# A PEER gate build whose row products read one input from PSUM, with GpSimd making some of the weight splits beside them

## The chip, the cores and the metric

One Trainium2 chip, one of its cores. The metric is the device time of one execution in microseconds (us). The kernel before ran three times: 1541.89, 1541.98 and 1545.73 us, median 1541.98.

## What is computed

A decoder block for 512 tokens of width 1024 in fp32: LayerNorm, a hybrid mixer (Mamba-2 heads and latent attention), LayerNorm, and a PEER expert mixer, LayerNorm. The change lies in the PEER part:

```
q = (xb @ w_query).reshape(T, 8, 2, 128)
s = einsum('thkd,hknd->thkn', q, sub_keys)          # scores of 2 x 128 keys per head
sv, si = top_k(s, 16);  cand = sv[0] + sv[1]        # 256 candidates per head
top_s, pos = top_k(cand, 16);  gate = softmax(top_s)
expert e = 128 * i + j                              # 128 experts per token (8 heads x 16)
act  = gelu(x . u_table[e])
out += gate * act * v_table[e]                      # 16384 experts in the tables
```

## The kernel before

The tokens are four blocks of 128. For the first 384 tokens, less 64, the kernel doesn't gather experts: it multiplies by the whole tables. "U" is x times u_table, in 128 chunks of 128 experts for 320 tokens (`u_half`, L1395, two halves a chunk); "V" is the gated activations times v_table, in 128 chunks (`v_chunk`). A dense gate matrix is made for this from the selected experts in `build_g` (L1199). The last 64 tokens of block 2 get their activations from gathered rows: 64 gathers of 128 rows of 4 KB (`ug_fetch`, L1125, issued on GpSimd) and 64 products, a row tile times x, summed along the row on VectorE (`ug_dots`, L1131, the instruction is L1134). Block 3 is gathered in the same way later, in `gather` (L1518; products L1549 and L1555), beside the V chunks.

fp32 products are made of three fp32r matmuls (`mm3`, L84: high x high, high x low, low x high). The weights come through one `Stream` (L94): a DMA on the SP queue fetches a raw 128 x 1024 tile (three raw buffers), ScalarE copies it to fp32r (the high part `wih`, L122), and a subtraction raw minus high gives the low part `wil` (L132), on the engine that `lo_on` names: VectorE, or GpSimd in some earlier stages. The next raw tile's DMA is issued only when the subtraction has freed its buffer. A U chunk's low part is made when the chunk two before it starts.

`build_g` runs 48 iterations (n), each for 8 token columns of 384. An iteration has, on VectorE, the one-hot tile `oj` (L1222) and the gate tile `g` (L1228) for the next iteration, then two of the 64 gathered products (n < 32 only); on TensorE 16 small matmuls (L1264, L1265) into a ring of four PSUM tiles (`pw`), which ScalarE copies out (L1267). On GpSimd each product is followed by the gather of the row tile four ahead, as its buffer is then free (four row buffers, `UROWS`). At n = 9 and 25, `g_head` (L1166) transposes the next block's indices and gates into a PSUM tile (`px`, a second ring of two); `digits` (L1180) reads it at n = 11 and 27, `g_low` (L1189) at n = 12 and 28.

The order of the work is written out by a planner at build time, not chosen on the chip. `drive` (L1458) steps the generator `build_g`; it keeps two clocks, `tm[0]` for TensorE and `tm[1]` for VectorE, in us, and inserts U halves (1.8 us each on the first clock) while the first is not ahead of the second. A U chunk's low part adds 1.2 us to the second clock (L1453). An iteration with n < 32 yields twice: ahead of its two products, where halves come only if the clocks ask for them, and behind them, where at least one half is put. `drive` also stops inserting U at chunk 76 (`AHEAD`) or 85 (`PRE - RES`). Chunks up to 88 that are left when the build ends are run right behind it, ahead of the first V chunk, with block 3's gathered products pumped in between; the V loop starts with 88 chunks of U done in any case.

[...] The x of the 64 tokens lies in a strided part of an SBUF tile (`UR["x"]`, two DMAs at L1493, issued on GpSimd).

Of the kernel before, what the change touches and what calls it, by code (L numbers as in the profile page):

```python
# [11 lines left out]
F32 = mybir.dt.float32  # L12
# [5 lines left out]
AF = mybir.ActivationFunctionType  # L18
# [48 lines left out]
def tile_block(ctx: ExitStack, tc: tile.TileContext, I, out):  # L67
# [6 lines left out]
    def pool(name, bufs=1, **kw):  # L74
        p = tc.alloc_tile_pool(name=name, bufs=bufs, **kw)
        opened.append(p)
        return p
# [15 lines left out]
    class Stream:  # L93
# [32 lines left out]
        def splits(self, m):  # L126
            while self.ns < min(m, len(self.srcs)):
                n = self.ns
                self.his(n + 1 + self.ha)
                r, h = self.raw.pop(n), self.hi.pop(n)  # L130
                l = self.tiles(n, 1)[:, :r.shape[-1]]
                self.lo(n).tensor_tensor(l, r, h, op=OP.subtract)  # L132
                self.w[n] = (h, l)
                self.ns += 1
                self.loads(n + 1 + self.rawb)
# [119 lines left out]
    items = []  # L255
    plan = items.extend
    lo_on = [V]

    wo_ = [I["wo"][k] for k in range(16)]
    ut_ = [I["ut"][i] for i in range(128)]  # L260
# [666 lines left out]
    close(psT)  # L927
    close(cs2)

    psX = pool("psX", bufs=2, space=PSUM)  # L930
    psW = pool("psW", bufs=4, space=PSUM)
    px = lambda: psX.tile([128, 512], F32, name="px")
    pw = lambda: psW.tile([128, 512], F32, name="pw")

# [196 lines left out]
    def ug_dots():  # L1131
        for n in range(UG):
            r = UR.pop(n)
            V.scalar_tensor_tensor(wide(r), wide(r), 1.0, UR["x"], op0=OP.mult, op1=OP.mult, accum_out=UR["hd"][:, n:n + 1])  # L1134
            ug_fetch(n + UROWS)
            yield 1.2
        A.activation(UR["hd"][UG:], UR["hd"][UG:], AF.Gelu)
        nc.scalar.dma_start(UR["w"][:, UG:], UR["hd"][UG:])
        A.activation(UR["w"][:, :UG], UR["hd"][:UG], AF.Gelu)
        close(ug)  # L1140
        more_act(pool("act2"))
        yield 0.1

    def ug_head():
        w, g = UR["w"], UR["g"]
        mx, r = UR["m"][:, 0:1], UR["m"][:, 1:2]
        V.tensor_tensor(w, w, g, op=OP.mult)
        V.scalar_tensor_tensor(g, w, -1.0, w, op0=OP.mult, op1=OP.max)
        yield 0.6
        V.tensor_reduce(mx, g, axis=AX.X, op=OP.max)  # L1150
        V.tensor_scalar(mx, mx, 1.0e-30, None, op0=OP.max)
        V.reciprocal(r, mx)
        yield 0.7
        V.tensor_scalar(w, w, r, None, op0=OP.mult)
        G.dma_start(scl[128 - UG:], mx)
        yield 0.3
        ps = px()
        T.transpose(ps[:, :UG], w, ident[:UG, :UG])
        gT = GT[2][1][:, 64 - UG // 2:]
        gv = ps[:, :UG].rearrange("p (k c) -> p k c", c=2)  # L1160
        A.activation(gT[:, :, 0], gv, AF.Copy, scale=GSC)
        yield 0.1
        V.scalar_tensor_tensor(gT[:, :, 1], gv, GSC, gT[:, :, 0], op0=OP.mult, op1=OP.subtract)
        yield 0.2

    def g_head(b):  # L1166
        ijg = IJG.pop(b)
        ps = px()
        for x, e in enumerate((1, 2, 0)):
            T.transpose(ps[:, x * 128:(x + 1) * 128], ijg[:, e].rearrange("p h k -> p (h k)"), ident)  # L1170
        jT = ijp.tile([128, 64, 2], F16, name="jT", bufs=2)
        gT = ijp.tile([128, 64, 2, 2], F16, name="gT")
        rT = ijp.tile([128, 8, 4, 2], F32, name="rT", bufs=2)
        pr = ps[:, :384].rearrange("p (e k c) -> p e k c", e=3, c=2)
        A.activation(jT, pr[:, 0], AF.Copy)
        A.activation(gT[:, :, 0], pr[:, 1], AF.Copy, scale=GSC)
        GT["ps"] = pr, b
        GT[b] = jT, gT, rT
# [20 lines left out]
    def build_g():  # L1199
# [44 lines left out]
        for n in range(48):  # L1244
# [45 lines left out]
            if b < 2:  # L1290
                if g == 9:
                    g_head(b + 1)
                if g == 11:
                    digits()
                    lump += 0.9
                if g == 12:
                    g_low()
                    lump += 1.1
            lump += (1.45 if n + 1 in LOWA else 1.95) if n < 47 else 0.1
            if n < 32:  # L1300
                keep, least[0] = least[0], 0
                yield lump
                least[0], lump = keep, 0.0
            for _ in range(2):
                lump += next(dots, 0.0)
            for _ in range({35: 2, 36: 1, 37: 1, 38: 1}.get(n, 0)):
# [141 lines left out]
    def step_u():  # L1448
        e = len(UO)
        u_half(un[0], e)  # L1450
        un[0] += e
        tm[0] += T_U / 2
        if not e and lo_on[0] is V:  # L1453
            tm[1] += 1.2

    un = [uc]
# [1 line left out]
    def drive(fill):  # L1458
        n = 0
        while True:  # L1460
            if (tm[0] <= tm[1] and len(aps) == 1 or n < least[0]) and un[0] < (PRE - RES if len(aps) > 1 else AHEAD):
                step_u()
                n += 1
                continue
            c = next(fill, None)
            if c is None:
                return
            tm[1] += c
            n = 0
# [29 lines left out]
    iaE = rt2.tile([128, 16, 16], F16, name="iaE")  # L1499
    nc.sync.dma_start(iaE.rearrange("p a b -> p (a b)"), I["ch"][:, 256:512])  # L1500
    lo_on[0] = V
    drive(stage2())
    close(rt2)
    close(rt)
# [101 lines left out]
    refill()  # L1606
    if UO:
        step_u()
    close(psW)
    close(psX)  # L1610

    psV = pool("psV", space=PSUM)
    va = [[psV.tile([128, 512], F32, name=f"va{b}{e}") for e in range(2)] for b in range(3)]
# [262 lines left out]
```

## Time and profile before

| | us |
|---|---|
| median of 3 runs | 1541.98 |
| the profiled execution, whole | 1543.65 |
| its span in the trace | 1541.9 |
| TensorE matmul busy | 1520.9 (99%) |
| VectorE busy | 1354.3 (88%) |
| ScalarE busy | 761.0 (49%) |
| GpSimd busy | 644.3 (42%) |

All times below are us from the start of the span. The first small matmuls of the build's iteration 0 are at 599.05, those of iteration 32 at 806.49, and the build's last PSUM tile is copied out by 854. [...]

### The profile page before, as it was taken

To read this page: it belongs to the slowest core of one execution; us is meant where nothing else is said; L and a number is where in the kernel's file an instruction comes from. 1 tells how busy PE (TensorE), PEld (TensorE's weight loads), DVE (VectorE), ACT (ScalarE), POOL (GpSimd) and SP (SyncE) were. 2 spreads that over 40 slices of the span, in tenths; PEclk is the share of its full clock that TensorE was granted. 3 is DMA by queue.
4 is the path that set the end of the run, shared out by engine and by line. 5 is a ranking of instruction groups with operands and counts; after the bars stand their busy time and mean duration, and the time that the engine had idled before them with its cause. 6 is when DMAs were issued, how large, how long until landed. Compare 5 with 4: busy or idle time off the path is not lost.

```text
span 1541.9 us, 24586 instructions
## 1 busy us (share of the span) xinstructions
PE 1520.9 (99%) x8664; PEld 1339.1 (87%) x8664; DVE 1354.3 (88%) x2641; ACT 761.0 (49%) x1415; POOL 644.3 (42%) x469
## 2 busy tenths in 40 slices
PE   9999999999999999999999999999999999999997
PEld 7787888888888999999999889999999788888886
DVE  8989768746799999999998689999988999999997
ACT  5574477742433445667666544444443344444442
POOL 0000032520244422444430566666666677766610
PEclk9999999999999999999999999999999999999999
DMA  6242122474422566999998999999999999999983
GB/s 253 96 155 100 57 71 59 118 253 151 140 89 81 158 205 220 350 337 366 365 325 290 376 401 382 387 386 391 395 380 387 377 381 377 390 387 384 366 298 150
DMA packets 153452, 417.59 MB, mean 271 GB/s; under 512 B 15200, under 2 KB 56560, under 8 KB 153072
## 3 DMA queue, kind: packets, MB, share of 16 engines
q1 hardware_dynamic: 95568, 210.34, 39.3%
q0 software_dynamic: 52352, 187.25, 32.6%
q10 hardware_dynamic: 5408, 18.43, 3.0%
q8 instruction: 68, 1.11, 0.3%
q14 instruction: 56, 0.46, 0.1%
HBM read 383.59 MB, written 30.21 MB: 268 GB/s over the span
## 4 chain that ended last, share of the span: by engine, by line
PE 83%; DVE 6%; DMA 6%; issue 3%; ACT 2%; POOL 1%; DVEq 0%; ACTq 0%; POOLq 0%
PE va L1671 9%; PE va L1668 9%; PE va L1667 9%; PE pu L85 9%; PE pu L87 9%; PE pu L86 9%; PE pw L85 3%; PE pw L86 3%; PE pw L87 3%; PE pa L86 3%; PE pa L87 3%; PE pa L85 3%; DMA wir<-ut 2%; DMA row<-v,ix 2%; DMA row<-u,ix 2%
## 5 line engine op out<-in xcount | busy, mean ns | idle before, releaser
L122 ACT ACTIVATE wih<-wir 128x1024 fp32r<-128x1024 f32 (+2 forms) x269 | 277.7, 1033 | 191.9 <-DMA wir<-ut 87.9
L132 DVE TENSOR_TENSOR wil<-wir,wih 128x1024 fp32r<-128x1024 f32 (+1 forms) x232 | 280.7, 1211 | 76.4 <-ACT wih L122 50.1
L87 PE MATMUL pu<-XT,wil 128*128 128x320 f32 x1000 | 309.9, 310 | 0.2
L1668 PE MATMUL va<-wil,Ph 128*128 128x512 f32 x726 | 283.3, 390 | 1.4 <-DVE wil L132 1.4
L1534 POOL DMA_INDIRECT row<-v,ix x128 | 220.1, 1719 | 102.1 <-DVE ac L1555 81.1
L85 PE MATMUL pu<-XT,wih 128*128 128x320 f32 x824 | 257.6, 313 | 1.0 <-ACT aout L1409 1.0
L86 PE MATMUL pu<-XT,wih 128*128 128x320 f32 x824 | 254.5, 309 | 0.0
L1534 POOL DMA_INDIRECT row<-u,ix x128 | 181.3, 1416 | 133.7 <-DVE row L1549 72.9
L1667 PE MATMUL va<-wih,Ph 128*128 128x512 f32 x486 | 189.2, 389 | 0.0
L87 PEld LDWEIGHTS pu<-XT,wil 128*128 128x128 f32 x1000 | 188.3, 188 | 0.7 <-DVE wil L132 0.7
L1555 DVE SCALAR_TENSOR_TENSOR ac<-row,hd,ac 128x1024 f32<-128x1024 f32 x128 | 164.1, 1282 | 2.5 <-DMA row<-v,ix 0.9
L1668 PEld LDWEIGHTS va<-wil,Ph 128*128 128x128 f32 x726 | 136.3, 188 | 29.6 <-DVE wil L132 2.5
L85 PEld LDWEIGHTS pu<-XT,wih 128*128 128x128 f32 x824 | 154.7, 188 | 3.1 <-ACT aout L1409 1.3
L1549 DVE SCALAR_TENSOR_TENSOR row<-row,XT 128x1024 f32<-128x1024 f32 x128 | 153.3, 1224 | 3.2 <-DMA row<-u,ix 3.1
L86 PEld LDWEIGHTS pu<-XT,wih 128*128 128x128 f32 x824 | 154.8, 188 | 1.5
L1128 POOL DMA_INDIRECT urow<-u,uix x64 | 97.0, 1516 | 139.9 <-DVE urow L1134 120.5
L1671 PE MATMUL va<-wih,Pl 128*128 128x512 f32 x486 | 149.9, 389 | 1.9 <-DVE Pl L1658 1.9
L132 POOL TENSOR_TENSOR wil<-wir,wih 128x1024 fp32r<-128x1024 f32 (+3 forms) x37 | 77.8, 2110 | 144.8 <-ACT wih L122 125.4
L1650 ACT ACTIVATE Ph<-P 128x384 fp32r<-128x384 f32 x121 | 62.7, 518 | 125.8 <-DVE P L1627 110.1
L1671 PEld LDWEIGHTS va<-wih,Pl 128*128 128x128 f32 x486 | 91.2, 188 | 21.3 <-DVE Pl L1658 2.3
L1667 PEld LDWEIGHTS va<-wih,Ph 128*128 128x128 f32 x486 | 91.2, 188 | 18.1
L122 ACT ACTIVATE wihx<-wir 128x1024 fp32r<-128x1024 f32 x67 | 70.9, 1058 | 66.5 <-DMA wir<-v 38.3
(507 smaller groups left out, 3335.7 us busy)
## 6 DMA issues: line engine op xcount, KB each, us to landing
wir<-ut SPq DMA_DIRECT2D x128, 512.0 KB
wir<-v SPq DMA_DIRECT2D x128, 512.0 KB
gt<-gsp SPq DMA_DIRECT2D x63, 256.0 KB
wir<-wo SPq DMA_DIRECT2D x26, 512.0 KB
gsp<-stg ACTq DMA_DIRECT2D x21, 448.0 KB
wir<-wf SPq DMA_DIRECT2D x18, 512.0 KB
wir<-wqr SPq DMA_DIRECT2D x16, 512.0 KB
asp<-aout SPq DMA_DIRECT2D x35, 160.0 KB
```

What stands on the lines that cost most here:

```text
L85: T.matmul(ps, lh, rh, start=start, stop=False)
L86: T.matmul(ps, lh, rl, start=False, stop=False)
L87: T.matmul(ps, ll, rh, start=False, stop=stop)
L122: A.activation(h, r, AF.Copy)
L132: self.lo(n).tensor_tensor(l, r, h, op=OP.subtract)
L1128: G.indirect_dma_start(out=UR[n], out_offset=None, in_=I["u"], in_offset=bass.IndirectOffsetOnAxis(ap=UR["ix"][:, n:n + 1], axis=0))
L1534: G.indirect_dma_start(out=R[s], out_offset=None, in_=I["u"] if s < 128 else I["v"], in_offset=bass.IndirectOffsetOnAxis(ap=ix3[:, s % 128 ...
L1549: V.scalar_tensor_tensor(wide(r), wide(r), 1.0, x3, op0=OP.mult, op1=OP.mult, accum_out=hd[:, s:s + 1])
L1555: V.scalar_tensor_tensor(ac, r, hd[:, s - 128:s - 127], ac, op0=OP.mult, op1=OP.add)
L1667: T.matmul(va[b][e], Ph[b], h[:, cs], start=c == 0, stop=False)
L1668: T.matmul(va[b][e], Ph[b], l[:, cs], start=False, stop=False)
L1671: T.matmul(va[b][e], Pl[b], h[:, cs], start=False, stop=c == 127)
```

## The change

The input x of the 64 gathered products is copied once by ScalarE into two PSUM banks (the two of `px`, which is closed ahead of the build), and the products read it there. `g_head` and `ug_head` take a tile of the `pw` ring instead, and `digits` and `g_low` move to n = 10 and 26. Where a U chunk starts at the first yield of an iteration with n < 32, its low part is made by GpSimd: VectorE first writes one column of the low tile (a memset of 128 x 1), so that GpSimd's subtraction starts where VectorE has come to that place in its order, just ahead of the two products; the planner's VectorE clock is not charged for it.

```diff
--- before.py
+++ after.py
@@ -129,7 +129,11 @@
                 self.his(n + 1 + self.ha)
                 r, h = self.raw.pop(n), self.hi.pop(n)
                 l = self.tiles(n, 1)[:, :r.shape[-1]]
-                self.lo(n).tensor_tensor(l, r, h, op=OP.subtract)
+                if beside[0]:
+                    V.memset(l[:, 0:1].bitcast(F32), 0.0)
+                    G.tensor_tensor(l, r, h, op=OP.subtract)
+                else:
+                    self.lo(n).tensor_tensor(l, r, h, op=OP.subtract)
                 self.w[n] = (h, l)
                 self.ns += 1
                 self.loads(n + 1 + self.rawb)
@@ -255,6 +259,7 @@
     items = []
     plan = items.extend
     lo_on = [V]
+    beside = [False]
 
     wo_ = [I["wo"][k] for k in range(16)]
     ut_ = [I["ut"][i] for i in range(128)]
@@ -927,8 +932,8 @@
     close(psT)
     close(cs2)
 
+    psW = pool("psW", bufs=4, space=PSUM)
     psX = pool("psX", bufs=2, space=PSUM)
-    psW = pool("psW", bufs=4, space=PSUM)
     px = lambda: psX.tile([128, 512], F32, name="px")
     pw = lambda: psW.tile([128, 512], F32, name="pw")
 
@@ -1131,7 +1136,7 @@
     def ug_dots():
         for n in range(UG):
             r = UR.pop(n)
-            V.scalar_tensor_tensor(wide(r), wide(r), 1.0, UR["x"], op0=OP.mult, op1=OP.mult, accum_out=UR["hd"][:, n:n + 1])
+            V.scalar_tensor_tensor(r, r, 1.0, UR["xp"], op0=OP.mult, op1=OP.mult, accum_out=UR["hd"][:, n:n + 1])
             ug_fetch(n + UROWS)
             yield 1.2
         A.activation(UR["hd"][UG:], UR["hd"][UG:], AF.Gelu)
@@ -1154,7 +1159,7 @@
         V.tensor_scalar(w, w, r, None, op0=OP.mult)
         G.dma_start(scl[128 - UG:], mx)
         yield 0.3
-        ps = px()
+        ps = pw()
         T.transpose(ps[:, :UG], w, ident[:UG, :UG])
         gT = GT[2][1][:, 64 - UG // 2:]
         gv = ps[:, :UG].rearrange("p (k c) -> p k c", c=2)
@@ -1165,7 +1170,7 @@
 
     def g_head(b):
         ijg = IJG.pop(b)
-        ps = px()
+        ps = pw()
         for x, e in enumerate((1, 2, 0)):
             T.transpose(ps[:, x * 128:(x + 1) * 128], ijg[:, e].rearrange("p h k -> p (h k)"), ident)
         jT = ijp.tile([128, 64, 2], F16, name="jT", bufs=2)
@@ -1290,17 +1295,16 @@
             if b < 2:
                 if g == 9:
                     g_head(b + 1)
-                if g == 11:
+                if g == 10:
                     digits()
                     lump += 0.9
-                if g == 12:
                     g_low()
                     lump += 1.1
             lump += (1.45 if n + 1 in LOWA else 1.95) if n < 47 else 0.1
             if n < 32:
-                keep, least[0] = least[0], 0
+                keep, least[0], beside[0] = least[0], 0, True
                 yield lump
-                least[0], lump = keep, 0.0
+                least[0], lump, beside[0] = keep, 0.0, False
             for _ in range(2):
                 lump += next(dots, 0.0)
             for _ in range({35: 2, 36: 1, 37: 1, 38: 1}.get(n, 0)):
@@ -1450,7 +1454,7 @@
         u_half(un[0], e)
         un[0] += e
         tm[0] += T_U / 2
-        if not e and lo_on[0] is V:
+        if not e and lo_on[0] is V and not beside[0]:
             tm[1] += 1.2
 
     un = [uc]
@@ -1499,6 +1503,11 @@
     iaE = rt2.tile([128, 16, 16], F16, name="iaE")
     nc.sync.dma_start(iaE.rearrange("p a b -> p (a b)"), I["ch"][:, 256:512])
     lo_on[0] = V
+    close(psX)
+    psG = pool("psG", space=PSUM)
+    UR["xp"] = psG.tile([128, D], F32, name="xp")
+    for e in range(2):
+        A.activation(UR["xp"][:, e * 512:(e + 1) * 512].rearrange("p (a b) -> p a b", b=64), UR["x"][:, e * 8:(e + 1) * 8], AF.Copy)
     drive(stage2())
     close(rt2)
     close(rt)
@@ -1606,8 +1615,8 @@
     refill()
     if UO:
         step_u()
+    close(psG)
     close(psW)
-    close(psX)
 
     psV = pool("psV", space=PSUM)
     va = [[psV.tile([128, 512], F32, name=f"va{b}{e}") for e in range(2)] for b in range(3)]
```

## Rows read from the trace of the kernel before

**Rows 1.** Busy time by stretch of us, the granted clock, the DMA share.

```profile
core 0: us, PE busy (x) PEld busy (x) DVE busy (x) ACT busy (x) POOL busy (x), PEclk, DMA share, GB/s
599.00:806.50 207.50, 204.88 (x1689) 200.64 (x1687) 199.45 (x275) 136.09 (x288) 92.92 (x68) 0.99 0.95 342
806.50:853.60 47.10, 47.10 (x461) 45.60 (x460) 40.66 (x49) 33.15 (x67) 2.46 (x5) 1.00 0.84 296
866.00:1186.00 320.00, 320.00 (x1707) 285.45 (x1706) 287.77 (x422) 140.80 (x255) 211.81 (x163) 1.00 1.02 389
1186.00:1240.00 54.00, 50.47 (x259) 43.07 (x258) 49.17 (x52) 19.86 (x35) 36.79 (x24) 1.00 1.01 376
```

**Rows 2.** TensorE's busy time and granted clock in two stretches of 2 us.

```profile
752.00:754.00 2.00, 2.00 (x10) 0.50 1.01 404
754.00:756.00 2.00, 2.00 (x11) 0.68 1.03 340
```

**Rows 3.** Waits in 599 to 806.5: who waited for whom, total, times, longest.

```profile
ACT wih L122 <- DMA wir<-ut: 22.2, 12, 4.6
DVE wil L132 <- ACT wih L122: 4.6, 4, 1.6
PE pu L85 <- ACT aout L1409: 2.6, 2, 1.6
DVE urow L1134 <- DMA urow<-u,uix: 1.0, 3, 0.5
```

**Rows 4.** Line L1288, all its instructions: columns of U already done, times 32.

```profile
L1288 DVE TENSOR_TENSOR acts<-acts,stg x10: 1086/1616/1628, 625.7 to 832.7; 128x1408 f32<-128x1408 f32 x7, 128x896 f32<-128x896 f32 x1, 128x1152 f32<-128x1152 f32 x1, 128x1280 f32<-128x1280 f32 x1
```

**Rows 5.** Timelines of GpSimd and ScalarE where x is fetched; a small DMA's wait.

```profile
527.16 1.70 POOL L1493 DMA_DIRECT2D XT<-xsp  x2
...
528.13 0.44 ACT L1406 ACTIVATE acts<-pu 128x320 f32<-128x320 f32 x1 [2.13 <-PE pu L87]
...
531.65 0.44 ACT L1406 ACTIVATE acts<-pu 128x320 f32<-128x320 f32 x1 [2.13 <-PE pu L87]
...
555.41 1.87 POOL L1128 DMA_INDIRECT urow<-u,uix  x1 [3.52 <-DMA uix<-p]
```

**Rows 6.** Timeline of VectorE around the first pair of products.

```profile
599.79 1.22 DVE L1134 SCALAR_TENSOR_TENSOR urow<-urow,XT 128x1024 f32<-128x1024 f32 x1
600.93 1.22 DVE L1134 SCALAR_TENSOR_TENSOR urow<-urow,XT 128x1024 f32<-128x1024 f32 x1
602.08 1.22 DVE L132 TENSOR_TENSOR wil<-wir,wih 128x1024 fp32r<-128x1024 f32 x1
603.22 0.69 DVE L1222 TENSOR_TENSOR oj<-iotaE,jT 128x1024 f16<-128x1024 f16 x1
```

**Rows 7.** Whole span, by group: a memset, inputs in PSUM, in SBUF.

```profile
L383 DVE MEMSET cu<- 128x3 f32 x12 | 0.7, 61 | 0.0
L976 DVE TENSOR_TENSOR XT<-px,XT 128x512 fp32r<-128x512 f32 x8 | 5.2, 687 | 1.3 <-ACT XT L975 1.3
L504 DVE TENSOR_TENSOR xdt<-xs,dtt 128x512 f32<-128x512 f32 x8 | 5.1, 685 | 0.0
```

**Rows 8.** Timeline of GpSimd and of VectorE beside two low parts.

```profile
397.57 4.78 POOL L132 TENSOR_TENSOR wil<-wir,wih 128x1024 fp32r<-128x1024 f32 x2 [81.16 <-ACT wih L122]
...
397.24 1.28 DVE L960 SCALAR_TENSOR_TENSOR xm<-hres,pu 128x512 f32<-128x512 f32 x2
...
400.56 1.81 DVE L188 SCALAR_TENSOR_TENSOR lma<-lmy,lmh 128x1 f32<-128x1 f32 x1
...
402.60 0.22 DVE L188 SCALAR_TENSOR_TENSOR lma<-lmy,lmh 128x1 f32<-128x1 f32 x1
```

**Rows 9.** A gather on GpSimd, and the product that waited for its row.

```profile
607.90 1.44 POOL L1128 DMA_INDIRECT urow<-u,uix  x1 [0.30 <-issue]
...
617.09 1.23 DVE L1134 SCALAR_TENSOR_TENSOR urow<-urow,XT 128x1024 f32<-128x1024 f32 x1 [0.51 <-DMA urow<-u,uix]
```

**Rows 10.** GpSimd's instructions by group, whole span: gathers of the build.

```profile
L1128 POOL DMA_INDIRECT urow<-u,uix x64 | 97.0, 1516 | 139.9 <-DVE urow L1134 120.5 <-issue 8.8 <-DMA urow<-u,uix 7.1
```

## The prediction

> **What bounds the kernel now.** I read the busy time by stretch first, then the waits of the build, then the timelines of VectorE and GpSimd inside it. The stretches show that TensorE is the clock of the whole kernel: 320.00 of 320 us busy from 866 to 1186, 47.10 of 47.1 in the build's last third, 204.88 of 207.5 in its first 32 iterations (n < 32), which the change rewrites [rows 1]. [...] The other hole is at 1186 to 1240, 54.00 - 50.47 = 3.5 us [rows 1].
>
> So shorter work on VectorE is worth nothing by itself. The most that can be had is the idle time that the change can reach, 2.6 + 1.7 + 3.5 = 7.8 us; the only way to lose is new idle time on TensorE. The question is therefore whether the other engines still keep up when the planner gives TensorE less to do in the build.
>
> In n < 32 all are close together: VectorE is busy 199.45 of 207.5 us and the DMA engines at a share of 0.95 [rows 1].
>
> **What the planner does with it.** I worked its two clocks through with the costs in the code. For the kernel before this gives 28, 36, 40 and then 44 chunks of U done at the gate multiplications; the rows have 896, 1152, 1280 and 1408 columns, 32 times these, so the working holds [rows 4]. For the change it gives: 38 U chunks in n < 32 in place of 48, of which 19 get their low part on GpSimd (the title counts 16), and 77 chunks at the end of the build in place of 85. The 19 stand in n = 2, 4 to 10, 13, 14, 17, 20 to 22, 25, 26 and 28 to 30. The U work that leaves the build is not saved: it runs behind it at the same price.
>
> **TensorE's floor.** A chunk takes 531.65 - 528.13 = 3.52 us [rows 5]. Iterations 0 to 31 take 806.49 - 599.05 = 207.4 us, without holes and slow clock 207.4 - 2.6 - 1.7 = 203.1. Ten chunks fewer: 203.1 - 35.2 = 167.9 us.
>
> **VectorE.** 48 subtractions become 19: 29 fewer at 602.08 - 600.93 = 1.15 us from start to start (a duration of 1.22 overlaps its neighbour) [rows 6], 33.3 us. Added: 19 memsets at 0.06 [rows 7], 1.1 us. The trace has no product of 1024 columns with an input in PSUM. With 512 columns such an instruction takes 687 ns, one with both inputs in SBUF 685 [rows 7], so the lower end is nothing; the pair of products with a PSUM input beside GpSimd came at 0.64 us each [rows 8], against half of 1.15, which bounds the extra at 0.07 per 512 columns, 0.14 x 63 = 9 us. A fixed extra per instruction wouldn't double with the columns, so I take 0.05 x 63 = 3 us. VectorE then needs 199.5 - 33.3 + 1.1 + 3 = 170.3 us (167 to 176), a little over TensorE's floor, with no wait in it. Before, it had about 6 us of waits [rows 3].
>
> [...]
>
> **DMA.** 0.95 x 207.5 = 197 us of the engines' time. Ten chunks fewer are 5.2 MB of weights and 1.6 MB of stored activations, at 342 / 0.95 = 360 GB/s 19 us: 178 us are left. At the later rate, 389 / 1.02 = 381 GB/s, what moved here, 71 MB less 6.8, takes 168 us [rows 1]. So DMA is level with TensorE or 10 us beyond it; I don't expect the waits for weights (22.2 us on ScalarE, 12 times [rows 3]) to go.
>
> **GpSimd, the step that decides.** A low part takes 4.78 / 2 = 2.39 us there [rows 8]; the two gathers of an iteration take 1.52 us each [rows 10] and about 0.30 of issue in front [rows 9]: 2.39 + 2 x 1.82 = 6.0 us an iteration where GpSimd has all three. On average it fits (19 x 2.39 + 64 x 1.82 = 162 us), in runs it doesn't. In n = 4 to 10 the planner gives TensorE 37.2 us by its clock, x 203.1 / 209.4 (real to planned in the kernel before) = 36.1 us, and GpSimd needs 7 x 6.0 = 42.0: 5.9 late. In n = 20 to 22 and 28 to 30 it is 18.0 against 15.7 each time, 2.3 late. Together 10.5 us. Queued behind a late low part are the two gathers, and for their rows wait the products two iterations on, with all of VectorE behind them. That cover is thin: one row was used 617.09 - 607.90 = 9.2 us after its gather was issued and VectorE still waited 0.5 us [rows 9], while the iterations shrink from 6.5 to 5.2 us, so two of them leave 10.5 less the pair itself.
>
> A low part that starts late also overhangs the products. What that does is in the trace: beside two low parts the instruction with one PSUM input ran unhindered, while one of a single column with two SBUF inputs took 1.81 us, to the end of the low part, in place of 0.22 [rows 8]. In the build that is `oj`, `g` or the next subtraction. [...]
>
> TensorE has up to two iterations of `oj` and `g` ahead of it, so the first microsecond or so of each run is absorbed: I take 8 of the 10.5 (3 to 16, the upper end with 19 x 6.0 + 13 x 5.2 = 182 against 168, and 2 more of waiting).
>
> **The rest.** *x into PSUM:* ScalarE's two copies wait for two DMAs that GpSimd issues at 527.2 to 528.9; a small one took 3.5 us to land, a gather 9.2 [rows 5, 9], so ScalarE goes on at 533 to 539, two copies of some 0.6 us included. TensorE has a second U tile and waits only when the evacuation of 531.65 is 3.5 us late, past 535.2: 0 to 4 us, taken as 1. *Transposes in `pw`:* the fifth tile after them waits until VectorE has read the transposes, two digits calls at up to 2 us; `digits` stands right behind the one-hot tile that TensorE needs anyway: 0 to 4, taken as 0.5. *After the build:* 11 chunks stand ahead of V in place of 3, 9 of them with products of block 3 pumped beside them in place of 1, some 15 of 256 done earlier. That thins the load at 1186 to 1240 by 6%; of the 3.5 us there I take 1.5 back (0 to 3.5).
>
> **Sum.** n < 32: 167.9 + 8 (GpSimd's runs; VectorE's excess of 2.4 lies inside them) + 2.6 + 1.7 (waits for weights and slow clock as before) = 180.2. With the moved chunks 180.2 + 35.2 - 207.4 = +8.0; + 1 + 0.5 - 1.5: +8.0 us on the span of 1541.9. The profiled execution took 1543.65, 1.7 above the median; on the median of 1541.98 it makes 1550.
>
> **Rivals.**
> 1. *The cover holds, and TensorE never waits* (faster, 0.23). Place: the second gather of an iteration with a GpSimd low part. If it is issued in time for its row to be there two iterations on, VectorE at its lower end (167) keeps pace, the 2.6 + 1.7 us go, and up to 3.5 later: 1534 to 1538. For it: VectorE waited only 1.0 us for rows, in 3 products [rows 3]. Against: 6.0 us of GpSimd in iterations of some 5. It decides at a row latency of about 8 us.
> 2. *Nothing but a shift* (0.17). The new idle time equals what the old stalls give back: 1540 to 1545.
> 3. *The raw tiles come late* (0.15). The next weight DMA goes out only when the subtraction has freed its raw buffer; on GpSimd that is 2.39 - 1.15 = 1.2 us later at best, 3 to 4 behind two gathers. Where ScalarE already waited up to 4.6 us for a tile [rows 3], 19 x 1.2 to 19 x 1.9 us (with the upper end of VectorE included) fall on TensorE: +16 to +32, 1558 to 1574. Products that hold GpSimd's reading after all would end here too.
> 4. *The change doesn't do what it says:* the planner's choice is fixed in the code, so only the title's 16 or my 19 can be off; 16 would take 1.5 us from the sum.
>
> **Chances.** The forecast (GpSimd late in its runs) 0.45, with its own range 1544 to 1557; the rivals 0.23, 0.17 and 0.15. 0.3% is 4.6 us, about what a measurement tells from no change: below 1537.4 faster, above 1546.6 slower. Faster: rival 1, 0.23, and a little of rival 2, 0.25. Same: most of rival 2 and the lower end of the forecast, 0.25. Slower 0.50. The range reaches from the middle of rival 1 to the lower part of rival 3: 1536 to 1565.
>
> **What would show it.** Right: gathers in n = 4 to 10 issued one after the other with no wait for a product; waits of products for rows well over 1.0 us; TensorE idle by some 10 us in the build; stretches of granted clock under 1. The product's start-to-start time tells the PSUM term (1.15 to 1.3). Wrong: TensorE busy throughout n < 32 and that stretch at 168 to 170 us (rival 1), or ScalarE's wait for weights far over 22 us with TensorE behind it (rival 3). [...]

## The result, and the profile after

The change is slower: median 1563.61 us of 4 runs (1561.61 to 1565.36) against 1543.86 for the kernel before (4 runs), ratio 1.0114 (95% interval 1.0076 to 1.0151). The profiled execution took 1561.61 us, its span is 1559.6: 17.7 us longer than before, where 8.0 was forecast. On the medians it is 19.8 us longer. The median lies at the upper end of the range, 1536 to 1565, and 6.6 us above the forecast's own range, 1544 to 1557.

First the stretches of the changed kernel (columns as in [rows 1]). Its iterations n < 32 are the first row; the others are the build's next part, the first part of the V stage, its start alone, a later part of it, and the place where x is fetched.

```profile
606.20:783.90 177.70, 172.58 (x1420) 164.04 (x1418) 163.09 (x257) 118.30 (x262) 115.98 (x78) 0.99 0.95 351
783.90:830.00 46.10, 44.16 (x416) 42.28 (x417) 41.28 (x51) 31.85 (x65) 7.04 (x13) 1.00 0.82 285
860.00:1180.00 320.00, 317.49 (x1711) 283.69 (x1710) 280.30 (x411) 145.32 (x263) 193.62 (x151) 1.00 1.00 380
860.00:890.00 30.00, 27.49 (x170) 25.34 (x169) 25.71 (x37) 13.33 (x24) 17.99 (x15) 1.00 1.03 412
1180.00:1240.00 60.00, 60.00 (x332) 54.23 (x331) 56.94 (x59) 23.14 (x38) 43.91 (x27) 1.00 1.02 387
520.00:560.00 40.00, 35.53 (x226) 35.26 (x225) 35.84 (x98) 18.12 (x27) 9.64 (x9) 0.91 0.55 149
```

By the busy times, TensorE idled 2.6 us before in n < 32 and, in the other stretches of [rows 1], only at 1186 to 1240. Now it idles 5.1 us in n < 32, 4.5 ahead of it, 1.9 behind it and 2.5 between 860 and 890. The hole at 1186 to 1240 is gone.

A correction to a mark of the prediction belongs here. Counting the gate matmuls, 16 to an iteration, the kernel before starts n = 32 at 803.74; 806.49 is n = 33. Its n < 32 therefore took 204.7 us, not 207.4, and the forecast for it, by the same steps, 204.7 - 2.6 - 1.7 - 35.2 = 165.2 and 8 + 2.6 + 1.7 = 12.3 on it, becomes 177.5 in place of 180.2. Expectations below that name such lengths were written with the old marks, up to an iteration off; the tables here use the counted ones.

With it the span splits at three starts: the first gate matmul, that of n = 32, the first V matmul.

| part of the span, us | before | after | difference | forecast |
|---|---|---|---|---|
| to n = 0 | 599.1 | 606.2 | +7.2 | +1 |
| n < 32 | 204.7 | 177.7 | -27.0 | -27.2 |
| n = 32 to the first V matmul | 60.2 | 101.6 | +41.4 | +35.2 + 0.5 |
| V to the end | 678.0 | 674.1 | -3.9 | -1.5 |

The parts of one kernel differ from run to run: two more profiles of the change (e5 and e12 below) have 176.8 and 179.0 in n < 32, and 676.7 and 674.8 from V to the end.

**Ahead of the build.** The timelines of ScalarE and GpSimd, after:

```profile
534.95 1.23 ACT L1510 ACTIVATE xp<-XT 128x512 f32<-128x512 f32 x2 [8.45 <-DMA XT<-xsp]
536.12 0.42 ACT L1410 ACTIVATE acts<-pu 128x320 f32<-128x320 f32 x1
...
527.67 1.71 POOL L1497 DMA_DIRECT2D XT<-xsp  x2
```

(`xp<-XT` are the two copies of x into PSUM, `XT<-xsp` the two DMAs that fetch x.) ScalarE stands in front of its copies for 8.45 us; x lands 7.3 us after GpSimd began to issue the two DMAs. No U tile (`pu`) is evacuated from then to 536.12. What that does to TensorE is in stretches of 2 us (after; the first busy time is TensorE's, the third number from the end its granted clock as a share of full speed):

```profile
532.00:534.00 2.00, 0.12 (x1) 0.00 (x0) 2.00 (x4) 0.00 (x0) 0.00 (x0) 1.00 0.88 173
534.00:536.00 2.00, 0.00 (x0) 0.00 (x0) 1.93 (x4) 1.02 (x2) 1.33 (x1) 0.75 0.81 229
536.00:538.00 2.00, 1.41 (x5) 1.41 (x6) 0.44 (x2) 2.00 (x5) 0.00 (x0) 0.50 0.80 184
538.00:540.00 2.00, 2.00 (x10) 2.00 (x9) 0.80 (x1) 1.98 (x2) 0.00 (x0) 0.50 0.67 141
540.00:542.00 2.00, 2.00 (x10) 2.00 (x10) 1.20 (x3) 1.97 (x3) 0.00 (x0) 0.55 0.66 238
```

It is idle from 532.12 to 536.59, 4.5 us, and comes back at a granted clock of 0.50, a U matmul every 0.267 us in place of 0.147, until shortly before 542: (1.41 + 2.00) x 0.50 + 2.00 x 0.45 = 2.6 us of full speed more. Together 7.1, the table's first line.

**In n < 32.** The waits after, 606 to 784 (columns as in [rows 3]):

```profile
ACT wih L122 <- DMA wir<-ut: 13.7, 8, 3.2
DVE urow L1139 <- DMA urow<-u,uix: 13.1, 15, 2.1
DVE wil L136 <- ACT wih L122: 1.1, 1, 1.1
ACT g L1237 <- DVE g L1233: 16.0, 11, 3.0
PE pu L85 <- ACT aout L1413: 1.6, 1, 1.6
PE pw L1269 <- DVE g L1233: 1.4, 1, 1.4
PE pw L1269 <- DVE wil L133: 1.0, 1, 1.0
```

Products wait for their rows 13.1 us in 15 places, against 1.0 in 3 [rows 3]. VectorE's 163.1 us of work, these 13.1 and 1.1 of waiting for a high part make 177.3 of the 177.7: VectorE is the bound here, and TensorE waits for its `g` and for what stands behind the late rows. (In the two other profiles of the change the rows wait 7.8 and 9.4 us.) GpSimd's timeline shows why rows are late, from 638 on:

```profile
638.53 2.41 POOL L134 TENSOR_TENSOR wil<-wir,wih 128x1024 fp32r<-128x1024 f32 x1 [2.02 <-ACT acts L1410]
641.09 0.94 POOL L1133 DMA_INDIRECT urow<-u,uix  x1 [0.15 <-issue]
642.34 1.35 POOL L1133 DMA_INDIRECT urow<-u,uix  x1 [0.30 <-DVE units L1219]
643.71 2.38 POOL L134 TENSOR_TENSOR wil<-wir,wih 128x1024 fp32r<-128x1024 f32 x1
646.26 1.22 POOL L1133 DMA_INDIRECT urow<-u,uix  x1 [0.16 <-issue]
647.78 0.95 POOL L1133 DMA_INDIRECT urow<-u,uix  x1 [0.30 <-issue]
648.75 2.40 POOL L134 TENSOR_TENSOR wil<-wir,wih 128x1024 fp32r<-128x1024 f32 x1
```

Low part, gather, gather, low part, with hardly anything between but issue, until 659.8: some 5.3 us an iteration (6.0 forecast), and none of these gathers waits for a product. VectorE beside it:

```profile
644.54 1.22 DVE L1139 SCALAR_TENSOR_TENSOR urow<-urow,xp 128x1024 f32<-128x1024 f32 x1
...
645.69 0.97 DVE L1227 TENSOR_TENSOR oj<-iotaE,jT 128x1024 f16<-128x1024 f16 x1
...
650.01 1.70 DVE L1227 TENSOR_TENSOR oj<-iotaE,jT 128x1024 f16<-128x1024 f16 x1
...
654.13 1.22 DVE L1139 SCALAR_TENSOR_TENSOR urow<-urow,xp 128x1024 f32<-128x1024 f32 x1 [0.68 <-DMA urow<-u,uix]
656.03 1.22 DVE L1139 SCALAR_TENSOR_TENSOR urow<-urow,xp 128x1024 f32<-128x1024 f32 x1 [0.67 <-DMA urow<-u,uix]
```

The products with x in PSUM run at 1.22 us through a low part. `oj`, two inputs in SBUF, takes 0.97 and 1.70 in place of 0.69 [rows 6] where the low part is still under way (643.71 + 2.38 = 646.09; 648.75 + 2.40 = 651.15). Soon after, two rows in turn are late.

How a late row reaches TensorE stands in the timelines of VectorE, ScalarE and TensorE around 643:

```profile
640.44 1.22 DVE L1139 SCALAR_TENSOR_TENSOR urow<-urow,xp 128x1024 f32<-128x1024 f32 x1 [0.92 <-DMA urow<-u,uix]
...
642.79 0.68 DVE L1233 TENSOR_TENSOR g<-tens,units 128x1024 f16<-128x1024 f16 x1
...
643.51 2.48 ACT L1237 ACTIVATE g<-g,rT 128x128 f16<-128x128 f16 x8 [5.04 <-DVE wil L133]
...
643.53 0.23 PE L1269 MATMUL pw<-g,oj 128*128 128x128 f16 x1 [1.02 <-DVE wil L133]
...
644.29 0.22 PE L1270 MATMUL pw<-g,oj 128*128 128x128 f16 x1
...
644.58 0.22 PE L1270 MATMUL pw<-g,oj 128*128 128x128 f16 x1
```

The product waits for its row, `g` behind it ends at 643.47, and TensorE stands until then. (The wait is put down to `wil`, a memset beside it; it is `g` that the matmul reads.) Where `g` has 1024 columns, ScalarE makes its other half in eight small copies (L1237), and TensorE now runs at their pace: one pair of gate matmuls in 0.29 us (644.29 to 644.58) in place of 2 x 0.0585. The waits don't list these steps, as each is short.

**Ahead of V.** Eleven U chunks now stand between the build and V. ScalarE's timeline there, after:

```profile
874.70 1.06 ACT L122 ACTIVATE wihx<-wir 128x1024 fp32r<-128x1024 f32 x1 [2.64 <-DMA wir<-ut]
878.88 1.06 ACT L122 ACTIVATE wih<-wir 128x1024 fp32r<-128x1024 f32 x1 [2.80 <-DMA wir<-v]
883.05 1.06 ACT L122 ACTIVATE wih<-wir 128x1024 fp32r<-128x1024 f32 x1 [2.78 <-DMA wir<-v]
```

These high parts come every 4.18 us (4.0 on average from 862.93 on), each after waiting for its raw tile, where a chunk takes TensorE 3.52. Block 3's rows are fetched beside them, and the DMA share of 860 to 890 is 1.03. TensorE loses 3.1 us between 860 and 886, counted as below. The SP queue and TensorE there:

```profile
873.71 0.33 SPq L104 DMA_DIRECT2D wir<-v  x1
...
882.47 0.33 SPq L104 DMA_DIRECT2D wir<-v  x1
...
880.32 0.41 PE L85 MATMUL pu<-XT,wihx 128*128 128x320 f32 x1 [0.40 <-ACT aout L1413]
...
885.54 0.50 PE L1676 MATMUL va<-wih,Ph 128*128 128x512 f32 x1 [1.44 <-ACT Ph L1659]
```

The raw tile whose DMA is issued at 873.71 is taken at 883.05, 9.3 us later. The DMA of 882.47 goes out when the subtraction of 881.22 has freed its buffer, 3.6 us after that buffer's tile was taken at 878.88. With three buffers that makes (9.3 + 3.6) / 3 = 4.3 us a tile, an estimate near the 4.18. TensorE's waits are named after ScalarE's evacuation and its `Ph`, which stand behind the waiting high parts in ScalarE's order.

### The profile page after: what moved, and what is told of

It reads as the page before. It is cut to its first block, busy times and chain, and to the rows that moved or that the text cites. A ratio compares the mean times of both kernels' runs of the same rounds, so it can differ in the third digit from the quotient of the medians.

```text
span 1559.6 us, 24660 instructions
## 1 busy us (share of the span) xinstructions
PE 1530.6 (98%) x8664; PEld 1343.6 (86%) x8664; DVE 1337.6 (86%) x2641; ACT 759.8 (49%) x1417; POOL 655.0 (42%) x488
## 4 chain that ended last, share of the span: by engine, by line
PE 79%; DMA 8%; DVE 7%; issue 3%; ACT 2%; POOL 1%; ACTq 0%; DVEq 0%; POOLq 0%
PE va L1677 10%; PE va L1676 10%; PE va L1680 10%; PE pu L85 7%; PE pu L87 7%; PE pu L86 7%; DMA urow<-u,uix 4%; PE pw L85 3%; PE pw L86 3%; PE pw L87 3%; PE pa L86 3%; PE pa L87 3%; PE pa L85 3%; DMA wir<-v 1%; PE pb L533 1%
## 5 line engine op out<-in xcount | busy, mean ns | idle before, releaser
L136 DVE TENSOR_TENSOR wil<-wir,wih 128x1024 fp32r<-128x1024 f32 (+1 forms) x218 | 263.6, 1210 | 91.4 <-ACT wih L122 45.9
L1543 POOL DMA_INDIRECT row<-v,ix x128 | 210.7, 1646 | 124.8 <-DVE ac L1564 100.8
L1543 POOL DMA_INDIRECT row<-u,ix x128 | 173.4, 1354 | 156.1 <-DVE row L1558 92.1
L1133 POOL DMA_INDIRECT urow<-u,uix x64 | 79.1, 1236 | 73.9 <-DVE urow L1139 60.8
```

The source lines that it names most:

```text
L1133: G.indirect_dma_start(out=UR[n], out_offset=None, in_=I["u"], in_offset=bass.IndirectOffsetOnAxis(ap=UR["ix"][:, n:n + 1], axis=0))
L1543: G.indirect_dma_start(out=R[s], out_offset=None, in_=I["u"] if s < 128 else I["v"], in_offset=bass.IndirectOffsetOnAxis(ap=ix3[:, s % 128 ...
```

## The experiments

Holes are counted alike in all kernels: over TensorE's matmul starts, the distance to the next start less the ordinary distance (0.147 us for a U matmul, 0.0585 for a gate matmul). Slow clock is in them. Without its holes n < 32 is 197.6 us in kernels with 72.5 U chunks done at n = 32, and 162.4 with 62.5: ten chunks less, 35.2 us. Of the change's 15.3 us in n < 32, some 6 are the steps at ScalarE's pace described above, 5.9 single waits over 0.25 us; before, there are none of the first and 2.9 of the second.

| | U chunks at n = 32 | holes to n = 0 | in n < 32 | n = 32 to V | V to end, us | span |
|---|---|---|---|---|---|---|
| before | 72.5 | 0.5 | 7.1 | 1.0 | 678.0 | 1541.9 |
| the change | 62.5 | 7.2 | 15.3 | 7.2 | 674.1 | 1559.6 |
| e1 late copy | 62.5 | 1.4 | 19.1 | 6.5 | 674.1 | 1557.6 |
| e2 no GpSimd low part | 72.5 | 0.6 | 4.1 | 2.1 | 676.7 | 1539.7 |
| e3 planner charged | 72.5 | 0.5 | 6.3 | 4.1 | 675.3 | 1542.1 |
| e4 products from SBUF | 62.5 | 0.5 | 42.4 | 6.6 | 675.1 | 1580.8 |
| e5 the change again | 62.5 | 7.1 | 14.5 | 7.6 | 676.7 | 1562.6 |
| e6 credit alone | 62.5 | 0.6 | 22.4 | 6.6 | 674.1 | 1560.4 |
| e7 low part behind the gathers | 62.5 | 0.9 | 39.1 | 6.7 | 675.1 | 1578.0 |
| e8 six rows | 62.5 | 1.0 | 9.6 | 10.6 | 675.3 | 1552.8 |
| e9 charged, six rows | 72.5 | 0.6 | 2.0 | 2.1 | 678.5 | 1539.4 |
| e10 planner charged again | 72.5 | 0.6 | 2.0 | 1.7 | 679.8 | 1540.5 |
| e11 late copy again | 62.5 | 0.5 | 17.8 | 6.4 | 676.1 | 1556.8 |
| e12 the change, third time | 62.5 | 7.6 | 16.6 | 7.9 | 674.8 | 1563.7 |

The theory: the planner hands U chunks out of the build for VectorE time that VectorE does not have, so TensorE waits. Rivals: GpSimd's place in the order alone costs the time; the PSUM inputs or the transposes do; the copy of x does. Four kernels with the late copy cross the two: chunks moved out of the build or not (e1 and e6, e2 and e3), low parts on GpSimd or not (e1 and e3, e2 and e6).

**e1: the copy of x made late.** The two copies go from ahead of `drive(stage2())` to where block 2's indices are ready, long after x has landed; the later experiments have this too, except e4, e5 and e12.

```diff
+            if b == 2:
+                for e in range(2):
+                    A.activation(UR["xp"][:, ...], UR["x"][:, ...], AF.Copy)
                 ug_index(p3)
 ...
-    for e in range(2):
-        A.activation(UR["xp"][:, ...], UR["x"][:, ...], AF.Copy)
     drive(stage2())
```

> The changed kernel, but ScalarE's two copies of x into PSUM stand some 20 us later in its order, just ahead of the first gathers, when the DMAs they wait for have long landed. My theory: of the 17.7 us lost, 7.0 are this wait (ScalarE idle 8.45 us for the DMA, TensorE 4.5 us behind it and then 2.4 us at the lower clock), so this kernel takes 1563.6 - 7 = 1556 to 1557.5 us, and TensorE has no hole at 530 to 545. Rival (the wait only moves time that VectorE needs anyway before the build): less than 2 us back, 1561.5 to 1564.

Measured: 1559.74 us (1559.12 to 1562.37), ratio 1.0115 (1.0091 to 1.0139). The hole is gone, TensorE is busy all of 520 to 560:

```profile
601.10:782.60 181.50, 171.59 (x1421) 163.76 (x1419) 166.48 (x258) 118.92 (x263) 117.67 (x78) 0.99 0.94 346
520.00:560.00 40.00, 40.00 (x275) 40.00 (x274) 39.59 (x104) 20.82 (x32) 11.84 (x9) 1.00 0.59 162
```

But n < 32 takes 181.5 where it took 177.7: part of the gain is given back there, and the time is above the 1556 to 1557.5 expected. How much it is, e11 and e12 measure on one chip.

**e2: no low part on GpSimd.** PSUM inputs and transposes stay; VectorE makes every low part, and the planner charges it.

```diff
-                keep, least[0], beside[0] = least[0], 0, True
+                keep, least[0], beside[0] = least[0], 0, False
```

> Late copy as in the first kernel, and no low part on GpSimd: VectorE makes all, and the planner charges them as before. Left of the change: products read x from PSUM, transposes in the ring of the gate products, digits earlier. My theory: what is left costs nothing, 1541 to 1545 us, products still 1.14 us from start to start and waits for rows about 1 us. Rival (the two PSUM banks and the shared ring cost something): 1547 to 1552, with TensorE waiting in iterations 10 to 12 and 26 to 28.

Measured: 1541.97 (1539.17 to 1551.53), ratio 0.9994 (0.9974 to 1.0014). The loss is gone, so neither the PSUM inputs nor the transposes in `pw` cost anything that shows.

**e3: the planner is charged.** GpSimd still makes low parts (16 then, by the trace), but each costs the VectorE clock its 1.2 us.

```diff
-        if not e and lo_on[0] is V and not beside[0]:
+        if not e and lo_on[0] is V:
             tm[1] += 1.2
```

> Late copy, low parts on GpSimd beside the products, but the planner charges VectorE for them as if it had made them. By its clocks 85 chunks of U are then done at the end of the build as in the kernel before, 16 of them with a GpSimd low part, never more than two iterations in a row. Theory: GpSimd is late only in long runs, so the waits for rows fall from 13.1 to under 5 us and TensorE stays covered: 1538 to 1545 us, perhaps 2 to 4 under the kernel before, as the stalls at 726 to 756 go. Rival (any low part ahead of the gathers makes rows late enough to hold TensorE): 1548 to 1554.

Measured: 1541.40 (1536.95 to 1548.05), ratio 0.9977 (0.9954 to 1.0000). Low parts on GpSimd do no harm that shows when the chunks stay in the build, though the products still wait 6.6 us for rows (under 5 expected; 4.5 in e10). This is the first half of the proof.

**e4: the products read SBUF again.** The change without the copy, the products as before; GpSimd's low parts and the planner stay.

```diff
-            V.scalar_tensor_tensor(r, r, 1.0, UR["xp"], ...)
+            V.scalar_tensor_tensor(wide(r), wide(r), 1.0, UR["x"], ...)
```

> The changed kernel without the copy into PSUM: the products read both inputs from SBUF while GpSimd makes its 19 low parts. By the port reading of my prediction (an instruction with two SBUF inputs was held 1.6 us beside a low part) the two products of such an iteration are held until the low part ends, about 2 us each time, 19 x 2 = 38 us on VectorE, of which 15 to 35 come through: 1563.6 - 7 + 15 to 35 = 1572 to 1592 us, products of 2 to 3.5 us in the trace. Rival (two fp32 inputs of 1024 columns share the port without loss): 1556 to 1558 us, as with the late copy alone.

The port reading named here is the 1.81 us against 0.22 of [rows 8]; what the two engines share is shown by no run.

Measured: 1583.62 (1580.39 to 1584.81), ratio 1.0262 (1.0236 to 1.0288). The timelines of VectorE and of GpSimd in e4 show one pair:

```profile
642.14 1.22 DVE L1139 SCALAR_TENSOR_TENSOR urow<-urow,XT 128x1024 f32<-128x1024 f32 x1
...
643.29 3.37 DVE L1139 SCALAR_TENSOR_TENSOR urow<-urow,XT 128x1024 f32<-128x1024 f32 x1
...
642.45 3.13 POOL L134 TENSOR_TENSOR wil<-wir,wih 128x1024 fp32r<-128x1024 f32 x1
```

The low part ends at 645.58, 2.29 after the first product makes way at 643.29; the second product ends at 646.66, 1.08 after the low part. They run one after the other. Over all of e4 a product takes 1.78 us and a low part 3.17 on average, against 1.22 and 2.41 in the change. So the PSUM input is what lets a product and a low part overlap.

**e5: the change once more**, beside e6 to e8, without an edit.

> The changed kernel as it is, on the chip of the next three. It sets the late copy's worth on one chip: from the runs so far 1563.6 against 1559.7 us, but on two chips. If the hole at 530 to 545 is wholly lost time it should be some 7 us above the late-copy kernel, 1565 to 1568; if the build's own waits take part of it back (late copy: other holes at 593 and 660), 3 to 4 us, 1562 to 1565.

Measured: 1563.57 (1561.09 to 1566.34), ratio 1.0114 (1.0090 to 1.0138), as the first time.

**e6: the credit alone.** VectorE makes all low parts again, but the planner still doesn't charge the 19.

```diff
-                if beside[0]:
-                    V.memset(l[:, 0:1].bitcast(F32), 0.0)
-                    G.tensor_tensor(l, r, h, op=OP.subtract)
-                else:
-                    self.lo(n).tensor_tensor(l, r, h, op=OP.subtract)
+                self.lo(n).tensor_tensor(l, r, h, op=OP.subtract)
```

> Late copy; VectorE makes every low part, but the planner still doesn't charge it for the 19 that start ahead of the products. So the order of U on TensorE is that of the change (77 chunks done at the build's end) with no work given to GpSimd. New theory: the loss is the planner's credit, U chunks taken out of the build for VectorE time that is not really saved. VectorE then needs 163 + 19 x 1.15 = 185 us for n < 32 where TensorE has 168: 1542 + 17 = 1556 to 1563 us, close to the 1559.7 of the late-copy kernel, and GpSimd's help was worth only the difference. Rival (GpSimd's lateness alone makes the loss): without it VectorE keeps up, 1542 to 1548.

Measured: 1562.55 (1561.28 to 1564.12), ratio 1.0110 (1.0090 to 1.0130). Its stretch n < 32 and its waits:

```profile
600.50:785.30 184.80, 176.80 (x1421) 167.78 (x1420) 181.68 (x258) 119.30 (x263) 67.22 (x59) 0.96 0.94 341
```
```profile
PE pw L1267 <- DVE g L1231: 4.9, 3, 2.4
DVE urow L1137 <- DMA urow<-u,uix: 1.5, 3, 0.9
```

Rows are in time (1.5 us), and VectorE is simply full: 181.7 of 184.8 us. The loss is as large with no low part on GpSimd at all. That is the second half: with the ten chunks out of the build the loss is there whoever does the subtractions, with them in the build (e2, e3) it is not. What VectorE lacks differs: time of its own in e6, rows in time in the change. What GpSimd's help gives back in n < 32 is 22.4 - 19.1 = 3.3 us, or 4.6 with e11; the ratios of e6 and e1 don't tell the two kernels apart.

**e7: the low part behind the two gathers.** GpSimd issues both gathers first, so that no row is delayed by a low part; the low part and the DMA of the next raw tile come after them.

```diff
                 if beside[0]:
-                    V.memset(l[:, 0:1].bitcast(F32), 0.0)
-                    G.tensor_tensor(l, r, h, op=OP.subtract)
+                    def later(l=l, r=r, h=h, n=n):
+                        G.tensor_tensor(l, r, h, op=OP.subtract)
+                        self.loads(n + 1 + self.rawb)
+                    behind.append(later)    # run after the pair of products
```

> Late copy; GpSimd's low part is queued behind the two gathers of its iteration, not ahead of the products. If late gathers cost the time, waits for rows fall from 11.6 to under 4 us and the kernel gains 4 to 8 us on the late-copy one: 1552 to 1556. If the hold of VectorE's instructions with two SBUF inputs is as dear as the late rows, each of the 19 low parts now holds oj, g or a subtraction by up to 2 us, and it stays at 1558 to 1566 with one-hot and gate instructions well over 0.69 and 1.22 us.

Measured: 1579.83 (1578.83 to 1581.84), ratio 1.0223 (1.0202 to 1.0243). Its waits, 600 to 800:

```profile
PE pu L87 <- POOL wil L136: 13.6, 7, 3.3
PE pw L1274 <- DVE g L1238: 6.1, 2, 4.4
DVE urow L1144 <- DMA urow<-u,uix: 4.3, 7, 1.3
ACT wih L122 <- DMA wir<-ut: 37.7, 14, 4.8
```

Rows wait 4.3 us instead of 11.6 (e1), and the kernel is 20 us slower than e1, outside both cases of the expectation: now TensorE waits for the low parts themselves, and the low part meets `oj` (1035 ns on average in n < 32, 814 in e1). The raw tiles come late too, 37.7 us of ScalarE's waits for 16.6 in e1, as their DMAs go out behind the gathers: the mechanism of the prediction's rival 3, which the change itself doesn't show in n < 32. Ahead of the products is the better place.

**e8: six row buffers in place of four**, to take the late rows away by themselves. The space comes from seven chunks' activations that then go through DRAM.

```diff
-KEEP = 53
+KEEP = 46
-REST = 8
+REST = 15
-UROWS = 4
+UROWS = 6
```

> Late copy with six row buffers in place of four, so a gather is issued three iterations ahead (seven activation tiles move from the first pool to the last to make room, so some more chunks go by DRAM). If rows that come late are what keeps VectorE from earning the planner's credit, its waits for rows go (11.6 to under 2 us) and TensorE's holes in n < 32 shrink from some 13 us to 5: 1550 to 1555. If GpSimd's overhang or the DMA load is the cause, 1556 to 1562.

Measured: 1554.51 (1553.88 to 1559.42), ratio 1.0066 (1.0041 to 1.0091). n < 32 in e8:

```profile
600.50:772.50 172.00, 169.26 (x1421) 163.46 (x1419) 169.32 (x258) 118.98 (x263) 114.77 (x76) 0.99 0.97 366
```

No product waits for a row, and the holes fall from 19.1 and 17.8 (e1, e11) to 9.6: the late rows are 8 to 10 us. VectorE is now busy 169.3 of 172.0 us: that, not TensorE's 162.4, is the floor. Part of it is `oj` held by low parts, 915 ns on average for 758 in the change. The holes grow to 10.6 between n = 32 and V, 4.7 of them one wait for a low part on VectorE, while a product of block 3 waited 8.6 us for its row.

**e9: e3 with six rows**, a try at a version that beats both.

```diff
 e3 and
-UROWS = 4
+UROWS = 6
 (KEEP 46, REST 15)
```

> The version that the runs point to: late copy, 16 low parts on GpSimd, the planner charging VectorE for them (TensorE keeps its U chunks in the build), and six row buffers so that late gathers hold nobody. TensorE's work outside its holes has been 1530 to 1533 us of span in all kernels so far; with holes of some 6 us left (slow clock after one stall, the first iterations without products) I expect 1536 to 1541 us, 0.995 to 0.998 of the kernel before. If the extra chunks that go by DRAM cost what the rows give back, it equals the charged kernel with four rows.

Measured: 1542.69 (1540.43 to 1548.22), ratio 0.9999 (0.9982 to 1.0015). Missed: the late rows cost nothing that shows once TensorE has its chunks (2.0 us of holes in n < 32 with six rows and, in e10, with four), so there was nothing to win.

**e10: e3 again**, for a narrower interval.

> The charged kernel with four rows again, beside the one with six on one chip: 0.9977 of before in its first runs, expected 0.996 to 0.999, 1540 to 1543 us.

Measured: 1540.42 (1536.60 to 1548.06), ratio 0.9978 (0.9964 to 0.9992): faster than the kernel before by 0.2%, at the edge of what these runs tell apart, as e3's interval reaches 1.0000 and e9's passes it. In n < 32:

```profile
600.30:799.90 199.60, 199.60 (x1661) 196.33 (x1660) 179.63 (x271) 134.37 (x287) 110.12 (x78) 1.00 0.95 350
```

TensorE never stops, and VectorE has 20 us to spare. In e2 it is busy 194.9 of 201.7 us: with 15 us taken off VectorE, TensorE's holes are 2.0 us here for 4.1 in e2, but 6.3 in e3, the same kernel, and the medians of the three (1541.97, 1541.40, 1540.42) are not told apart. That GpSimd's help gains anything is not shown.

**e11 and e12: e1 and the change on one chip**, to price the copy.

> The late-copy kernel beside the change itself on one chip. The hole at 530 to 545 costs 7 us of span in both profiles of the change, but the medians differed by 4 only, on two chips. If the hole is wholly lost: 6 to 8 us under the change. If the build takes half of it back by more late rows (holes of 20.3 us between 600 and 820 in the late-copy profile against 16 to 18 in the change): 3 to 4 us.

> The changed kernel, as the partner of the late-copy kernel on this chip: 1562 to 1566 us, 1.010 to 1.013 of the kernel before.

Measured: 1559.68 (1557.33 to 1562.59), ratio 1.0107 (1.0089 to 1.0126), and 1564.59 (1561.17 to 1566.89), ratio 1.0129 (1.0108 to 1.0150). The late copy is worth 4.9 us by the medians (3.9 with e5 in e12's place), between the cases of the expectation: 7 us of holes go ahead of the build, and n < 32 loses 1.2 of them again (16.6 to 17.8).

## Why the prediction was right, and where its sum was short

**Right.** TensorE was the bound, nothing off VectorE was worth anything that shows by itself, and the loss is new idle time on TensorE. The planner's working was exact: 19 low parts on GpSimd (14 and 5 instructions), ten chunks fewer at n = 32. The stretch n < 32, the step called decisive, came to 177.7 us for 177.5 forecast. Most of its signs are there: GpSimd almost without a pause from 638.5 to 659.8, rows late by 13.1 us for 1.0 [rows 3], `oj` stretched beside a low part (0.97 and 1.70 us in place of 0.69), as in [rows 8], a granted clock under 1 (0.50 at 740 to 742). The "some 10 us" of idle time are 5.1 by the busy time and 8.2 more than before by the holes (15.3 for 7.1). Rival 1 (the cover holds) falls with these rows, rival 2 (a shift) with the 17.7 us, rival 4 with the 19 low parts. Rival 3 falls in n < 32: the wait of `wih` for raw tiles is 13.7 us, for 22.2 before [rows 3], and no wait of TensorE for a low part is among the rows.

**Where it was luck.** The sum gave 1550; the range holds 1563.61 only because its upper end was set by rival 3, whose mechanism the change doesn't show in n < 32. That n < 32 agrees to 0.2 us is luck in part: the other two profiles have 176.8 and 179.0; by the holes the floor was 2.8 us too high (165.2 for 162.4) and the waits 3.0 too low (12.3 for 15.3); and VectorE's work was 163.1 us where 170.3 was forecast, 2.8 of the difference by the mark, 3 by the PSUM term.

**Right in size, too narrow in cause.** I put the 8 us down to GpSimd's queue. e8 confirms that price: rows in time save 8 to 10 us. But e6, without any low part on GpSimd, loses as much, since VectorE then lacks the time itself. The cause behind both is the credit in the planner: it brings TensorE's floor down to VectorE's work (162.4 and 163.1), and then whatever delays VectorE falls on TensorE. With 20 us to spare (e10) late rows cost nothing that shows. The prediction had the parts, VectorE's need beside TensorE's floor, but put VectorE's excess "inside" GpSimd's 8 us and looked for the loss only in GpSimd's runs.

**The step that was mis-sized: the copy of x**, "0 to 4 us, taken as 1". It took 7.1 in the profile, 3.9 to 4.9 by the medians. I counted the cover from the evacuation of 531.65 [rows 5], so to 535.2. In the trace of after the evacuation due near 528 already stood behind the copies, so TensorE ran out at 532.1. And I charged no slow clock after a hole, though [rows 2] show it: 2.6 us here.

**The step that was missing: what the moved chunks do where they go.** "After the build" had only a gain in it, 1.5 us; it came to 3.9 in these two profiles, and to 2.6 on average (677.7 with 72.5 chunks, 675.0 with 62.5). Beside it stand 6.2 us of holes more from n = 32 to V (7.2 for 1.0). Of the 7.2, 2.4 lie between 786 and 804, 1.3 of it one wait for the `g` of a VectorE still behind, and 3.1 where raw tiles come late beside block 3's gathers. Kernels with ten chunks fewer all have 6.4 to 10.6 there, those with 72.5 have 1.0 to 4.1. That it is the DMA engines that are short at the start of V rests on ScalarE's waits, the 9.3 us of a raw tile and the share of 1.03; VectorE's subtractions, which start 1.3 us after the high part is done (881.22), lengthen the same loop, and no run changes either alone, so this stays open.

**Smaller terms.** The product with an input in PSUM has no extra: 1215 ns on average, 1221 the median from SBUF in e4, 1.14 us from start to start, so 0 for the 3 us taken. Transposes: no wait of TensorE for a `pw` tile above 0.4 us in n < 32. Two SBUF inputs beside a low part: e4 agrees with [rows 8], 3.13 us for a low part of 2.40 and 3.37 for a product of 1.22. The 2.6 and 1.7 us that the sum takes over from before are the two waits for an evacuation [rows 3] and the slow clock behind the second, 2 x 0.50 + 2 x 0.32 from the granted 0.50 and 0.68 [rows 2]; counted as holes, n < 32 has 7.1 there.

Together: 8.0 + 6.2 (copy) + 0.2 (n < 32) + 5.7 (n = 32 to V) - 2.4 (V) = 17.7.

## What to carry to other kernels

Where a planner trades two engines against each other, taking work off one engine should credit it only after a trace shows that the receiving engine and its queue keep pace: here 16 low parts with the charge left in are within 0.2% of the kernel before, 19 without it 1.1% slower. On a kernel whose bound engine is at 99%, the relief of another engine is worth at most the bound engine's holes (2.0 to 7.1 us in n < 32 of the kernels with 72.5 chunks), so price first what the relief makes the planner do. With both engines planned to the same length (162.4 and 163.1 us here), the delays of one became idle time of the other; with 20 us to spare they didn't: leave slack to the engine that waits for DMAs. An engine that keeps to the order of its program, as ScalarE did here, should not be given a copy until its transfer has landed: its wait of 8.45 us reached the bound engine one buffer earlier than the timeline before suggests, as a hole of 4.5 us, and 2.6 us of slow clock followed.

## What the runs showed that was not expected

A VectorE product with one of its two inputs in PSUM runs at the pace of one from SBUF (1215 and 1221 ns) and through a GpSimd subtraction, where a product from SBUF and the subtraction take strict turns (3.37 and 3.13 us, alone 1.22 and 2.40). After 4.5 us without a matmul, TensorE's granted clock was 0.50 for 4 us and 0.55 in the 2 us after; after the 1.4 us hole that ends at 783.95 it stayed at 1.00. The length of the hole alone doesn't tell: it was 0.50 at 740 to 742, after one of 1.6 us, and in e12 TensorE went on at its full pace, a U matmul every 0.147 us, after one of 2.7 us that ends at 786.64.
